# The output projection of a hybrid encoder layer as seven block products in place of eight

## The chip, the core and the metric

The kernel runs on one core of a Trainium2 chip. The metric is device time in microseconds (us) for one execution. The engines are TensorE (PE; PEld is its weight load), VectorE (DVE), ScalarE (ACT), GpSimd (POOL) and SyncE (SP, which issues the transfers). Each works through its own list of instructions in order.

## What is computed

One layer on 1024 tokens of 1024 channels, all in float32. Only the last lines matter here:

```
y_a = attn * silu(z_a)
y_b = h * silu(z_b)
m = sigmoid(g_a + b_merge[0]) * (y_a @ w_ba) + sigmoid(g_b + b_merge[1]) * (y_b @ w_bb)
out = m @ w_out
return layer_norm(ALPHA * x + out, ln_g, ln_b)
```

`y_a` and `y_b` are 1024 x 512, `w_ba` and `w_bb` 512 x 1024, `m` 1024 x 1024 and `w_out` 1024 x 1024.

## The kernel before

A float32 product is made from three products of fp32r numbers. Each operand is split into a high part (a copy, cast to fp32r) and a low part (the rest, by `lo_of`, L127). `mm3` (L130) issues three matmuls for each 128-row piece of the contraction: high x high, low x high, high x low. Nearly every matmul of the kernel has line L134, so one goes by the tile's name.

The kernel has an earlier part (embedding layer norm, input projection, gated recurrence) and the attention, which the change leaves as they are but for the shape of one tile. The order of the instructions on every engine is the order in which the program writes them. What follows attention is this:

**The merge of the branches** (tiles `mb`, loop at L1316). `m` is built transposed: for j = 0..7 (128 channels each) and n = 0, 1 (512 tokens each) a group of twelve matmuls forms 128 x 512 of `y_a @ w_ba` in a PSUM bank. `b_load`, `b_split` fetch and split the weights for the next j (ACT makes the high part, L900, POOL the low one); `g_load` fetches the gate. `merge` (L1300) then lets DVE multiply by the gate (`b_gate`, L1020) and add the other branch's part `late["m", j, n]` (L1302), ACT make the high part `mh` (L1304), and `merge_lo` lets DVE make the low part `ml` one step later. The other branch's part was formed during attention (`filler`), and so its tiles `m` lie in SBUF. Beside that, ACT and POOL split the rows of `w_out` into `wo` (L1344 and L128), 128 x 1024 at a time.

**The output projection** (tiles `o`, `o_product` at L1365, loop at L1390). For each of the eight tiles i of 128 tokens, and for each half of the columns, 24 matmuls (eight k, three each) with `mh` and `ml` as weights and `wo` as the moving operand fill a bank. DVE adds `ALPHA` times the layer's input `z` (L1399) and takes statistics (L1402, L1404). `newton` (L1375) has ACT take a root (L1378) and DVE refine it. For all tiles but the last, ACT then scales `z` (L1408), POOL multiplies by the gain and adds the bias (L1409, L1410), each over 1024 columns, and SP stores the tile (L1411). The last tile's second half is formed in two pieces of 256 columns, and DVE does all of its end (L1416, L1421), with four stores (L1422).

Banks come in turn from eight: two tags `mb`, `s`, `tp` of two banks each, and two banks `acc` of the attention.

## Time and profile before

| | us |
|---|---|
| median of 3 runs (676.55 to 676.87) | 676.69 |
| the profiled execution | 676.07 |
| its span, first to last instruction | 674.3 |

| engine | busy us in the span | share |
|---|---|---|
| PE | 663.7 | 98% |
| DVE | 498.9 | 74% |
| ACT | 364.5 | 54% |
| POOL | 354.4 | 53% |

A row of the profile's groups or of its timeline gives line, engine, operation, the tile written and those read, the shape, and times. In a group's row `busy, mean ns` is followed by the idle time ahead of it and who ended it. In the timeline the first two numbers are the start and the length in us from the span's start, and square brackets hold idle time ahead. Line numbers are those of the kernel before, unless a run of another kernel is shown.

### The profile page before, as it was taken

The page shows a single profiled execution, that of the slowest core. Times are in us where ns is not written, and L with a number is a line of the kernel's source. Part 1 is how long each engine was busy: PE and PEld are TensorE (multiplying, and loading weights), DVE is VectorE, ACT ScalarE, POOL GpSimd, SP SyncE. Part 2 cuts the span into 40 slices and gives each one's busy share as a digit, 9 for nine tenths or more (in the row PEclk, how much of TensorE's full clock was granted, in tenths as well). Part 3 has the DMA queues.
Part 4 walks back from the last instruction along what each step waited for, and adds up shares of the span by engine and source line. Part 5 has one row for each costly group of instructions (what it writes and reads, how often), then busy time and mean ns, then how long its engine had stood idle before and what let it go on. Part 6 is the DMA issues. An engine that isn't in the chain of part 4 may idle for free.

```text
span 674.3 us, 9352 instructions
## 1 busy us (share of the span) xinstructions
PE 663.7 (98%) x3189; PEld 554.3 (82%) x3189; DVE 498.9 (74%) x835; ACT 364.5 (54%) x615; POOL 354.4 (53%) x261
## 2 busy tenths in 40 slices
PE   8999999999999999999999999999999999999995
PEld 7888888888888887888788888888888888888884
DVE  6978876985998699879968785477788787443334
ACT  6555433357786676669576634477777555210110
POOL 5898263433676575567647544115255456334432
PEclk9999999999999999999999999999999999999999
DMA  8746616033344033531543557998794467412211
GB/s 322 246 152 228 209 41 221 36 125 109 126 143 150 22 108 110 172 126 48 202 172 124 172 186 261 339 332 308 251 317 146 163 232 280 170 62 94 93 63 62
DMA packets 48990, 113.40 MB, mean 168 GB/s; under 512 B 5088, under 2 KB 9776, under 8 KB 47408
## 3 DMA queue, kind: packets, MB, share of 16 engines
q1 hardware_dynamic: 48912, 112.81, 48.0%
q8 instruction: 25, 0.41, 0.2%
q14 instruction: 21, 0.17, 0.1%
q10 hardware_dynamic: 32, 0.01, 0.0%
HBM read 77.11 MB, written 35.68 MB: 167 GB/s over the span
## 4 chain that ended last, share of the span: by engine, by line
PE 76%; DVE 9%; issue 4%; POOL 1%; ACT 1%; DMA 1%; SPq 0%; DVEq 0%; POOLq 0%
PE a L134 28%; PE o L134 13%; PE mb L134 13%; PE s L134 11%; PE acc L1145 4%; PE s L1099 3%; PE pt L1121 3%; PE g L794 2%; POOL ht_l L128 1%; DVE ws_l L128 1%; DVE wa_l L128 1%; DMA a_2f<-in_w_s_dram 1%; DVE uc L752 1%; ACT ht_h L312 1%; DVE s_12f L384 0%
## 5 line engine op out<-in xcount | busy, mean ns | idle before, releaser
L134 PE MATMUL a<-ht_h,ws_h 128*128 128x512 f32 x136 | 53.1, 391 | 0.0
L134 PE MATMUL a<-ht_h,ws_l 128*128 128x512 f32 x136 | 53.0, 389 | 0.0
L134 PE MATMUL a<-b_h,wa_l 128*128 128x512 f32 x136 | 53.0, 389 | 0.0
L134 PE MATMUL a<-ht_l,ws_h 128*128 128x512 f32 x136 | 52.9, 389 | 0.0
L134 PE MATMUL a<-b_h,wa_h 128*128 128x512 f32 x136 | 52.9, 389 | 0.0
L134 PE MATMUL a<-b_l,wa_h 128*128 128x512 f32 x136 | 52.9, 389 | 0.0
L134 PE MATMUL o<-wo_h,ml 128*128 128x512 f32 (+1 forms) x136 | 51.2, 377 | 0.0
L134 PE MATMUL o<-wo_l,mh 128*128 128x512 f32 (+1 forms) x136 | 51.2, 376 | 0.0
L134 PE MATMUL o<-wo_h,mh 128*128 128x512 f32 (+1 forms) x136 | 51.2, 376 | 0.0
L1109 DVE CUSTOM_DVE_ANT_0 sc<-s,bias 128x384 f32<-128x384 f32 (+1 forms) x64 | 33.3, 522 | 21.5 <-PE s L1099 14.1
L1399 DVE SCALAR_TENSOR_TENSOR z<-z,o 128x512 f32<-128x512 f32 (+1 forms) x17 | 11.2, 656 | 51.1 <-PE o L134 51.1
L1129 ACT CAST pt_h<-pt 128x384 fp32r<-128x384 f32 x64 | 29.0, 453 | 25.3 <-PE pt L1121 17.3
L1409 POOL TENSOR_TENSOR z<-z,gb 128x1024 f32<-128x1024 f32 x7 | 16.8, 2397 | 48.6 <-ACT z L1408 48.6
L1114 ACT ACTIVATE p<-sc,summ 128x384 f32<-128x384 f32 (+1 forms) x64 | 37.8, 591 | 5.5 <-DVE summ L1109 5.3
L1378 ACT ACTIVATE sd<-mv,eps_z 128x1 f32<-128x1 f32 x8 | 2.4, 294 | 67.1 <-DVE mv L1404 67.1
L128 DVE TENSOR_TENSOR pt_l<-pt,pt_h 128x384 fp32r<-128x384 f32 x64 | 33.2, 519 | 2.1 <-ACT pt_h L1129 1.6
L326 PE MATMUL v<-wv,b_h 128*128 128x512 f32 x128 | 32.8, 398 | 0.2 <-ACT b_h L279 0.2
L902 POOL CAST wb_h<-wb 128x512 fp32r<-128x512 f32 x9 | 7.0, 778 | 49.3 <-DMA wb<-in_w_bb_dram 49.3
L128 POOL TENSOR_TENSOR ht_l<-t,ht_h 128x512 fp32r<-128x512 f32 x16 | 22.0, 1408 | 19.9 <-ACT ht_h L312 19.9
L1099 PE MATMUL s<-ks,qs 128*128 128x384 f32 (+1 forms) x128 | 31.5, 327 | 0.0
L134 PEld LDWEIGHTS a<-ht_h,ws_h 128*128 128x128 f32 x136 | 25.5, 188 | 5.9 <-issue 0.4
L1121 PEld LDWEIGHTS pt<-ident,p 128*128 128x128 f32 x176 | 23.1, 140 | 8.5
(455 smaller groups left out, 2192.4 us busy)
## 6 DMA issues: line engine op xcount, KB each, us to landing
ks<-k_d SPq DMA_DIRECT2D x8, 1024.0 KB, 8.3
h_d<-x SPq DMA_DIRECT2D x8, 512.0 KB, 5.0
v_d<-vs SPq DMA_DIRECT2D x8, 512.0 KB, 3.5
q_d<-q SPq DMA_DIRECT2D x8, 512.0 KB, 3.0
ga_d<-ga SPq DMA_DIRECT2D x16, 256.0 KB, 2.2
gb_d<-gb SPq DMA_DIRECT2D x16, 256.0 KB, 2.4
k_d<-k SPq DMA_DIRECT2D x8, 512.0 KB, 3.4
qs<-q_d SPq DMA_DIRECT2D x8, 512.0 KB, 5.2
```

What stands on the lines that cost most here:

```text
L128: eng.tensor_tensor(lo, full, hi.bitcast(F32), ALU.subtract)
L134: PE.matmul(o, a, b, start=first and i == 0, stop=last and i == len(prods) - 1, skip_group_check=not (first and last))
L326: PE.matmul(vos[i][:], a, wv[kind == "w"][k][:], start=vn[i] == 0, stop=vn[i] == 23)
L794: PE.matmul(o[:, n, :], w[:, 2 * d + b, :], us[b][:, n * HALF:(n + 1) * HALF], start=z == 0, stop=z == 1)
L1099: PE.matmul(o[:, :P * len(near(t))], q[:, t * P:(t + 1) * P], k[:, z, keys], start=z == 0, stop=z == 1)
L1109: V.tensor_tensor_reduce(s[:, :w], o[:, :w], heads[h][2][:, b0:b0 + w], -1.0, 3.0e38, ALU.add, ALU.min, accum_out=sums[h][0][:, t:t + 1])
L1114: A.activation(probs[h % 2][t][:], scs.pop((h, t))[:, :w], AF.Exp, bias=sums[h][0][:, t:t + 1], scale=-1.0, accum_out=sums[h][1][:, t:t + 1])
L1121: PE.transpose(tp[:, n * P:(n + 1) * P], probs[h % 2][t][:, z * P:(z + 1) * P], ident[:])
L1129: A.copy(pt[0][:, span(b)], tps[h, b][:, :P * len(near(b))])
L1145: PE.matmul(acc[g][:, d:d + w], vvs[h // 2][:, b, h % 2, :], pt[:, a:a + w], start=b in (1, 6) and z == 0, stop=z == 1 and b == (4, 7)[g])
L1399: V.scalar_tensor_tensor(z[:, cols], z[:, cols], ALPHA * TWICE, o, ALU.mult, ALU.add)
L1409: G.tensor_tensor(z[:], z[:], gb2[:, 0, :], ALU.mult)
```

## The change

The 1024 x 1024 product is cut into two by two blocks of 512 and done by seven block products (Winograd's form) in place of eight. With A = `m` (rows: two halves of the tokens, columns: two halves of the channels) and B = `w_out`:

- left operands: a11, a12, a22, s1 = a21 + a22, s2 = s1 - a11, s3 = a11 - a21, s4 = a12 - s2
- right operands: b11, b21, b22, t1 = b12 - b11, t2 = b22 - t1, t3 = b22 - b12, t4 = b21 - t2
- products: a11 b11, a12 b21, s2 t2, s1 t1, s4 b22, s3 t3, a22 t4

Each product is done for four pairs p of token tiles (p and p + 4) in turn: a product for one p is twelve matmuls of 512 columns. Two banks serve each p, X and W. DVE reads X after a11 b11, after s2 t2 has been summed in, and again after s3 t3 and a22 t4; W likewise. `z` is now four quarters of 512 columns per pair, to which DVE adds what it reads.

The left sums are formed in the merge: DVE writes s3 over the bank of n = 1 (j < 4), and s2 and s4 over the bank that a22 came from. The right sums t1 to t4 are made by DVE from SBUF pieces of `w_out` of 128 x 512. ACT makes the high parts; the low parts of the right operands and of s1 are POOL's, the others DVE's. The tile `ya` becomes 16 tiles, so that its places can be taken over one by one. Steps are numbered by slots: 0 to 15 are the sixteen groups of the merge, 16 to 43 the 28 products. A table gives the jobs of each slot, which the program writes ahead of that slot's matmuls. The first product's low parts of b21 are in slots 16 to 19; those of t2 in 18 to 21.

A row tile's end (`finished`) now has ACT and POOL work on two halves of 512 columns, with two stores. The last tile's end works in the banks.

```
-    acc = [pst.tile([P, HALF], F32, name=f"acc{g}") for g in range(2)]
+    acc = [pst.tile([P, HALF], F32, tag=f"acc{g}", name=f"acc{g}") for g in range(2)]
...
+    RING = ("mb", "mb", "s", "tp", "acc0", "s", "tp", "acc1")
...
+    def merge(slot):
+        j, n = divmod(slot, 2)
+        c, o, m = j % 4, got[slot], late["m", j, n]
         b_gate(0, j, n, o)
+        if j < 4 and n:
+            V.tensor_tensor(m[:], o[:], m[:], ALU.add)
+            minus(o[:], late["m", j, 0][:], m[:])
+        else:
+            V.tensor_tensor(o[:], o[:], m[:], ALU.add)
+
+    def split(slot):
...
+        if name == "a22":
+            high(name, c, o[:], late["mp"], f"m{j}1")
+            V.tensor_tensor(late["m", c, 1][:], late["m", c, 1][:], o[:], ALU.add)
+        else:
+            high(name, c, o[:], ap, f"{name}h{c}")
+        if n == 0:
+            A.copy(m[:], o[:])
...
+    def second(c, o):
+        minus(o[:], late["m", c, 1][:], late["m", c, 0][:])
+        high("s2", c, o[:], late["mp"], f"m{c}0")
+
+    def fourth(c, o):
+        low("s2", c, o[:], ap, f"s2l{c}")
+        minus(o[:], late["m", c + 4, 0][:], o[:])
+        high("s4", c, o[:], late["mp"], f"m{c + 4}0")
+
+    def fourth_lo(c, o):
+        low("s4", c, o[:], wop, f"s4l{c}")
...
+    for slot in range(16):
+        j, n = divmod(slot, 2)
+        if slot > 1:
+            jobs.setdefault(slot + 1, [])[:0] = [lambda s=slot: merge(s), lambda s=slot: split(s)]
+        job(slot + 2, split_lo, slot)
+        if n and j >= 4:
+            job(slot + 2, lambda c, s: second(c, got[s]), j - 4, slot)
+            job(slot + 3, lambda c, s: fourth(c, got[s]), j - 4, slot)
+            job(slot + 4, lambda c, s: fourth_lo(c, got[s]), j - 4, slot)
...
+    for c in range(4):
...
+        job(2 * c + 3, t1, c)
+        job(2 * c + 4, lambda c: w_high("b11", c, wop, f"b11h{c}"), c)
+        job(2 * c + 5, lambda c: w_low("b11", c, raw["b11", c], wop, f"b11{c}"), c)
...
+        job(16 + c, lambda c: low("b21", c, raw["b21", c][:], yap, f"y1{c}1", G), c)
+        job(16 + c, lambda c: z_load(c, 0, 0, ev, "z", bufs=5), c)
...
+        job(17 + c, t2, c)
+        job(17 + c, t4, c)
+        job(17 + c, lambda c: w_high("t2", c, yap, f"y1{c}0"), c)
+        job(18 + c, lambda c: w_low("t2", c, raw["t2", c], yap, f"y0{c}1"), c)
+        job(18 + c, lambda c: high("s1", c, late["m", c, 1][:], yap, f"y0{c}0"), c)
...
+        job(20 + c, lambda c: w_low("s1", c, late["m", c, 1], late["mp"], f"m{c}1"), c)
+        job(21 + c, t3, c)
...
+    def finished(p, r):
+        mv = mean_var(p, r)
+        sd, ve = newton(mv, f"{p}{r}", iter(()))
+        V.tensor_scalar(ve[:, 2:3], mv[:, 0:1], -1.0, sd[:], ALU.mult, ALU.mult)
+        for n in range(2):
+            z = zs[p, r, n]
             A.activation(z[:], z[:], AF.Identity, bias=ve[:, 2:3], scale=sd[:])
+            G.tensor_tensor(z[:], z[:], gbs[0, n][:], ALU.mult)
+            G.tensor_tensor(z[:], z[:], gbs[1, n][:], ALU.add)
+            SP.dma_start(out[p + 4 * r][:, halves[n]], z[:])
...
+    LAST = [("s3", "t3", 0), ("s3", "t3", 1), ("a22", "t4", 0), ("s3", "t3", 2), ("a22", "t4", 1), ("s3", "t3", 3),
+            ("a22", "t4", 2), ("a22", "t4", 3)]
+    PLAN = [("a11", "b11"), ("a12", "b21"), ("s2", "t2"), ("s1", "t1"), ("s4", "b22")]
+    plan = [(a, b, p) for a, b in PLAN for p in range(4)] + LAST
...
+    for n, (a, b, p) in enumerate(plan[:-1]):
+        jobs.setdefault(17 + n, []).insert(0, lambda a=a, p=p: EVAC[a](p))
```

## The prediction, made before the changed kernel was run

> **What bounds the kernel now.** I read the page's head first, then stages, then the chain of the last stages in order of time.

> ```profile
> span 674.3 us, 9352 instructions
> PE 663.7 (98%) x3189; PEld 554.3 (82%) x3189; DVE 498.9 (74%) x835; ACT 364.5 (54%) x615; POOL 354.4 (53%) x261
> ```

> TensorE is busy for 98% of the span. An average does not say what a change in one stage is worth, so here are the busy times by stage (columns: stretch, length, PE, PEld, DVE, ACT, POOL, granted clock, DMA share, GB/s):

> ```profile
> 535.20:578.80 43.60, 43.60 (x193) 35.98 (x193) 33.97 (x50) 21.37 (x33) 27.78 (x16) 1.00 0.78 278
> 578.80:622.00 43.20, 43.20 (x192) 35.77 (x192) 16.03 (x36) 6.78 (x9) 16.79 (x7) 1.00 0.18 69
> 622.00:666.10 44.10, 44.10 (x218) 37.34 (x216) 16.86 (x43) 6.15 (x8) 19.16 (x8) 1.00 0.20 77
> 666.10:674.30 8.20, 0.02 (x1) 0.00 (x0) 4.79 (x15) 0.29 (x1) 0.00 (x0) 0.80 0.24 80
> ```

> The first row is the attention branch's projection (tiles mb), the next two the output projection (o), the last the tail. In the first, DVE is already busy 34.0 of 43.6 us; in the second and third DVE and POOL have half their time free. The chain of work that ended last, over these stages:

> ```profile
> 535.19 43.59 PE mb L134 x192
> 578.77 87.36 PE o L134 x408
> 666.14 0.02 issue
> 666.16 0.43 DVE z L1399
> ...
> 670.26 0.79 DVE z L1421 x2
> ```

> Nothing but TensorE up to 666.13, then a DVE tail. So matmuls taken out of o are worth their full time, as long as TensorE never waits and the end stays as short.

> **Unit.** 192 matmuls in 43.59 us: 0.227 each. I call twelve of them, 2.724 us, a slot: slots 0 to 15 are mb, and the output projection follows. Its 408 are 360 of 512 columns (81.7 us) and 48 of 256 columns, (87.36 - 81.7) / 48 = 0.118 each.

> **Matmuls removed.** Seven products for four token pairs are 28 slots, 16 to 43; the last is split in halves: 324 x 0.227 + 24 x 0.118 = 76.4 us. That is **-11.0 us**: without a wait, TensorE would end at 655.1.

> **DVE work added in the mb stage.** Before, each slot gives DVE three instructions (gate, add, low part). The changed code adds a difference in the bank for s3, an added right half for a22, two differences and two low parts for s2 and s4, and t1 to t4 from SBUF weights. These rows show what DVE pays:

> ```profile
> 540.53 0.69 DVE L128 TENSOR_TENSOR ya_l<-attn,ya_h 128x512 fp32r<-128x512 f32 x1 [0.69 <-ACT ya_h L1199]
> 541.14 0.69 DVE L1020 SCALAR_TENSOR_TENSOR mb<-g,mb 128x512 f32<-128x512 f32 x1
> 541.86 0.70 DVE L1302 TENSOR_TENSOR mb<-mb,m 128x512 f32<-128x512 f32 x1
> 543.21 0.69 DVE L128 TENSOR_TENSOR ml<-mb,mh 128x512 fp32r<-128x512 f32 x1 [0.66 <-ACT mh L1304]
> ...
> 545.15 0.69 DVE L1020 SCALAR_TENSOR_TENSOR mb<-g,mb 128x512 f32<-128x512 f32 x1
> 545.87 0.70 DVE L1302 TENSOR_TENSOR mb<-mb,m 128x512 f32<-128x512 f32 x1
> 546.48 0.68 DVE L128 TENSOR_TENSOR ml<-mb,mh 128x512 fp32r<-128x512 f32 x1
> 547.07 0.69 DVE L1020 SCALAR_TENSOR_TENSOR mb<-g,mb 128x512 f32<-128x512 f32 x1
> ```

> Start to start, 0.72 us where an instruction uses what the one ahead wrote, 0.60 where not. DVE reaches the first merge at 541.14, with slot 2 running: it begins over 5 us behind, and before it catches up because three instructions take 1.93 of 2.72 us. In the changed order each slot from 2 to 11 has four (about 2.6 us: no catching up), and slots 12 to 17 have 6, 5, 6, 5, 6, 6 (up to 4 us): it falls further behind.

> What waits for it: in the order of the changed kernel, POOL's low part of b21's third block stands behind that of t2's first block, and b21's fourth behind t2's second. t2 comes from DVE behind all of the above, and product a12 x b21 needs b21's fourth low part in its first slot, slot 20. Up to that t2, DVE has 2 + 4 + 9x4 + 28 + 6 + 4 = 80 instructions. 34 gaps have the second using the first's tile (0.72: 24.5 us), 45 do not (27.0), the last lasts 0.69, one early wait for ACT's high part 0.6. That is 52.8 us.

> Fifteen of the 80 read two SBUF tensors. Their collisions with POOL show where both did so before:

> ```profile
> 534.43 2.56 POOL L1183 TENSOR_TENSOR za<-za,rsb 128x512 f32<-128x512 f32 x2 [8.40 <-DMA rsb<-rs_d]
> 536.93 1.76 POOL L128 TENSOR_TENSOR wb_l<-wb,wb_h 128x512 fp32r<-128x512 f32 x1
> 544.72 1.29 POOL L128 TENSOR_TENSOR wb_l<-wb,wb_h 128x512 fp32r<-128x512 f32 x1 [6.03 <-ACT wb_h L900]
> ...
> 535.92 1.61 DVE L1198 TENSOR_TENSOR attn<-attn,za 128x512 f32<-128x512 f32 x1
> ```

> The DVE instruction ended 0.54 after POOL's, at 537.5, having lost 0.92; POOL's next lost 0.47. So one waits for the other's end. Bounds for fifteen: 0 (none meets) to 13.8 us (all lose 0.92). POOL has one instruction per slot in slots 4 to 12 and some at 17 and 18; laying the two queues side by side, six meet, at about 0.45: 2.7 us.

> [...]

> t2's second block is then done at 541.14 + 52.8 + 2.7 = 596.6. ACT's high part (row below), POOL's low part of t2 (1.29) and of b21 (1.29, plus 0.45 for meeting DVE's next difference) bring 600.3. TensorE, unhindered, would want it after eleven matmuls of slot 20: 535.19 + 20 x 2.724 + 11 x 0.227 = 592.2. **+8.1 us.** Some of it appears earlier: the weight split for mb (L900 on ACT, then POOL) now stands behind ACT's high part of s3 in the queue, which waits for DVE, so slots 6 and 14 should lose some 1.7 us each and slot 20 the rest, about 4.5. As DVE never waits for TensorE there, the total is set by DVE's queue. If there are no meetings at all it is 5 us. Then TensorE ends at 600.3 + 0.2 + 22 x 2.724 + 2.8 = 663.3, 2.8 earlier than before.

> ```profile
> L1304 ACT CAST mh<-mb 128x512 fp32r<-128x512 f32 x16 | 9.4, 588 | 20.3 <-DVE mb L1302 20.3
> L900 ACT CAST wb_h<-wb 128x512 fp32r<-128x512 f32 x7 | 4.4, 622 | 0.0
> ```

> ACT gains no more than four casts of 0.6 us per slot, under 2.72; it only passes DVE's lateness on. POOL has two low parts of 1.29 per slot in slots 18 to 29, due four slots or more ahead: covered, unless meetings add over about 4 us.

> **Loads.** The 4 MB of w_out come as 256 KB pieces at a similar pace; the 16 loads of z move from slots 9 on to 16 and later, one slot or more ahead of use, where the DMA share was 0.18. I cost them at nothing. TensorE's slot 17 to 20 cover them; if that fails, DVE's adds shift.

> **The end.** Rows finish in another pattern: four row tiles become ready in slots 33 to 36, three more in 39, 41 and 43. Each needs two multiplies and two adds of 512 columns on POOL, in place of two instructions of 1024. The early rows with this very pattern, and one tile of before from DVE's add to POOL:

> ```profile
> 30.83 5.29 POOL L259 TENSOR_TENSOR x<-x,gb 128x512 f32<-128x512 f32 x4 [1.05 <-ACT x L253]
> ...
> 589.69 0.69 DVE L1399 SCALAR_TENSOR_TENSOR z<-z,o 128x512 f32<-128x512 f32 x1 [4.02 <-PE o L134]
> ...
> 592.72 1.25 ACT L1408 ACTIVATE z<-z,ve,sd 128x1024 f32<-128x1024 f32 x1 [1.04 <-DVE ve L1407]
> ...
> 594.04 2.40 POOL L1409 TENSOR_TENSOR z<-z,gb 128x1024 f32<-128x1024 f32 x1 [12.47 <-ACT z L1408]
> ```

> Seven tiles at 5.25 (5.29 less the overlap) are 36.75 us. From slot 32's end to TensorE's end there are only 10 x 2.724 + 2.8 = 30.05 us. POOL starts 4.35 - 0.55 (half the width on ACT) = 3.8 after slot 32, so it ends 3.8 + 36.75 - 30.05 = 10.5 us after TensorE, at 673.8. At half of a 2.40 instruction (1.20) it would be 33.6 us, 7.4 after. SP keeps its order, so the last tile's four stores, ready near 668, queue behind POOL's last store:

> ```profile
> 669.89 1.79 SPq L1422 DMA_DIRECT2D out_dram<-z  x4
> ```

> Five issues at 0.45, the last at 675.65; before, the last issue (671.35) stood 2.95 ahead of the span's end: 678.6. The tail is thus 15.3 us in place of 8.2: **+7.1**.

> **Sum:** -11.0 + 8.1 + 7.1 = +4.2; rounded, span 678.6, time 676.07 + 4.3 = 680.4. The profiled execution was 0.6 below the median of the runs; I give **680.5**.

> **Rivals.**
> - *DVE keeps up* (faster). If b21's low part lands by 592.2, only the tail is paid: 676.07 - 11.0 + 7.1 = 672.2. DVE's 80 instructions would need 0.595 us each at most with no meeting; faster by over 0.2% needs a total wait under 2.5 us, 0.625 each. The rows' 0.60 and 0.72 speak against. Chance 0.09.
> - *POOL is not the end*: DVE's own tail is (8.2): 673.3. It needs POOL at 1.10 us an instruction; rows show 1.29. 0.04.
> - *No meetings*: 2.7 + 0.45 less: 677.3, within the bound. 0.12.
> - *More waits*: meetings slow POOL's 26 low parts so that slots 24 and 28 wait too: 3 to 4 us more, 684. 0.07.
> - *The clock drops*. After the last matmul the granted clock fell:

> ```profile
> 668.00:670.00 2.00, 0.00 (x0) 0.00 (x0) 2.00 (x7) 0.00 (x0) 0.00 (x0) 1.00 0.00 0
> 670.00:672.00 2.00, 0.00 (x0) 0.00 (x0) 1.05 (x3) 0.00 (x0) 0.00 (x0) 0.73 0.54 176
> 672.00:674.30 2.30, 0.00 (x0) 0.00 (x0) 0.00 (x0) 0.00 (x0) 0.00 (x0) 0.50 0.23 75
> ```

> The fall to half was near 670.9, 4.8 us after the last matmul. Slot 20's longest gap is about 3.5 us, so I expect none; a gap of 4.8 would cost, at half clock for as long, 2.4 us: 682.9. Chance 0.08. [...]

> That seven products are not what is issued is excluded: the changed list holds 60 fewer matmuls, as counted.

> **Chances and range.** Forecast 0.60 (677.9 to 683). 0.2%, 1.35 us, is about what can be told from no change. Faster 0.13 (first two rivals), same 0.12, slower 0.75. Range 675.4 to 684.0: it leaves out the faster cases and about 0.06 above.

> **What would show it.** Right: TensorE waits for wb's low part around slots 6 and 14, and for b21's in slot 20, about 8 us in all; DVE without a gap from 541 to about 608; POOL back to back over the last 36 us, ending some 10 us after TensorE, with the last four stores behind it. Wrong: no waits on TensorE ahead of slot 21, or a chain that ends on DVE; waits for z or weights by DMA, which I cost at nothing.

## The result, and the profile after

| | before | changed |
|---|---|---|
| median of 4 runs, us | 676.66 (676.55 to 676.87) | 686.37 (685.94 to 687.03) |
| profiled execution, its span | 676.07, 674.3 | 686.13, 684.3 |

The changed kernel is slower: ratio 1.0144, 95% interval 1.0126 to 1.0162. Forecast were 680.5 us and a range up to 684.0. The sign was right, and the time lies above the range.

The head of the changed kernel's page:

```profile
span 684.3 us, 9463 instructions
...
PE 658.1 (96%) x3129; PEld 545.7 (80%) x3129; DVE 535.9 (78%) x888; ACT 384.8 (56%) x662; POOL 383.0 (56%) x299
```

60 matmuls fewer, and yet PE is busy for only 5.6 us less, partly since some matmuls ran at half clock (0.43 us from start to start behind 604.86, in place of 0.227). The stages, with the same columns as before:

```profile
535.20:578.80 43.60, 40.45 (x175) 31.77 (x173) 39.06 (x57) 20.29 (x37) 17.43 (x13) 1.00 0.69 236
...
601.00:604.00 3.00, 0.00 (x0) 0.00 (x0) 2.90 (x5) 1.99 (x4) 2.88 (x2) 1.00 0.00 0
604.00:607.00 3.00, 2.88 (x8) 2.29 (x9) 2.91 (x4) 1.30 (x4) 2.92 (x3) 0.58 0.00 0
...
672.00:684.30 12.30, 0.00 (x0) 0.00 (x0) 3.32 (x11) 0.00 (x0) 7.12 (x6) 0.53 0.36 128
```

TensorE has holes in the merge (40.45 of 43.6 us; it was full before), stands still from 601 to 604 while DVE and POOL are busy for nearly all of it, and then runs 3 us at a granted clock of 0.58. What TensorE waited for, in sum, number and longest, and where:

```profile
PE w L134 <- POOL b21l L128: 3.6, 2, 3.4
PE mb L134 <- ACT wb_h L900: 2.3, 2, 1.4
PE mb L134 <- POOL wb_l L128: 1.7, 2, 0.9
```

```profile
578.41 0.49 PE L134 MATMUL mb<-ya,wb_h 128*128 128x512 f32 x1 [0.85 <-ACT wb_h L900]
579.76 0.50 PE L134 MATMUL mb<-ya,wb_l 128*128 128x512 f32 x1 [0.85 <-POOL wb_l L128]
...
604.12 0.52 PE L134 MATMUL w<-b21l,a12h 128*128 128x512 f32 x1 [3.38 <-POOL b21l L128]
```

These are the tiles and slots of the forecast (6, 14 and 20), 7.6 us in sum against "about 8". That match is of the gaps alone. By the times from one matmul's start to the next, the six waits cost 8.8 us, and matmuls that ran at half clock behind slot 14 or started up again behind a wait (0.33 us to the next start behind 579.76 and 604.12) some 2.5 more, so TensorE was about 11 us late in slot 20. The queue behind the last wait, on DVE and then POOL:

```profile
542.15 0.69 DVE L1021 SCALAR_TENSOR_TENSOR mb<-g,mb 128x512 f32<-128x512 f32 x1
...
544.72 0.69 DVE L128 TENSOR_TENSOR a11l<-mb,a11h 128x512 fp32r<-128x512 f32 x1 [1.14 <-ACT m L1346]
...
569.10 0.69 DVE L1342 TENSOR_TENSOR m<-m,mb 128x512 f32<-128x512 f32 x1 [0.65 <-ACT a22h L1317]
...
598.82 1.45 DVE L1324 TENSOR_TENSOR t<-wb,t 128x512 f32<-128x512 f32 x1
```

```profile
597.18 1.30 POOL L128 TENSOR_TENSOR t2l<-t,t2h 128x512 fp32r<-128x512 f32 x1 [9.72 <-ACT t2h L1317]
...
602.35 1.71 POOL L128 TENSOR_TENSOR b21l<-wb,b21h 128x512 fp32r<-128x512 f32 x1
...
678.09 1.26 POOL L1490 TENSOR_TENSOR z<-z,gb 128x512 f32<-128x512 f32 x1
```

t2's second block (598.82) ends at 600.27, where 596.6 was forecast; b21's fourth low part ends at 604.06, where 600.3 was. TensorE's last matmul ends at 668.95 (forecast 663.3), POOL's last addition 10.4 us after it (10.5), the span 15.35 after it (15.3). SP's own queue shows why the span goes on after POOL: the last tile's four stores are issued behind POOL's last store.

```profile
645.53 34.18 SPq L1491 DMA_DIRECT2D out_dram<-z  x14
679.80 1.86 SPq L1594 DMA_DIRECT2D out_dram<-z  x4
```

So three facts carry the difference: a loss of about 11 us up to slot 20, a stretch at half clock behind it, and a tail that is about 7 us longer. The experiments take them one by one.

### The profile page after: what moved, and what is told of

Its sections match the earlier page's. It is cut to its first block, busy times and chain, and to the rows that moved or that the text cites. A ratio compares the mean times of both kernels' runs of the same rounds, so it can differ in the third digit from the quotient of the medians.

```text
span 684.3 us, 9463 instructions
## 1 busy us (share of the span) xinstructions
PE 658.1 (96%) x3129; PEld 545.7 (80%) x3129; DVE 535.9 (78%) x888; ACT 384.8 (56%) x662; POOL 383.0 (56%) x299
## 5 line engine op out<-in xcount | busy, mean ns | idle before, releaser
L134 PE MATMUL a<-ht_h,ws_h 128*128 128x512 f32 x136 | 53.1, 391 | 0.0
L134 PE MATMUL a<-ht_h,ws_l 128*128 128x512 f32 x136 | 53.0, 390 | 0.0
L134 PE MATMUL a<-b_h,wa_l 128*128 128x512 f32 x136 | 53.0, 389 | 0.0
L134 PE MATMUL a<-b_h,wa_h 128*128 128x512 f32 x136 | 52.9, 389 | 0.0
L134 PE MATMUL a<-ht_l,ws_h 128*128 128x512 f32 x136 | 52.9, 389 | 0.0
L134 PE MATMUL a<-b_l,wa_h 128*128 128x512 f32 x136 | 52.9, 389 | 0.0
L134 PE MATMUL mb<-ya,wb_h 128*128 128x512 f32 x128 | 41.4, 402 | 2.3 <-ACT wb_h L900 2.3
L128 POOL TENSOR_TENSOR wb_l<-wb,wb_h 128x512 fp32r<-128x512 f32 x16 | 21.9, 1372 | 26.6 <-ACT wb_h L900 25.9
L128 DVE TENSOR_TENSOR pt_l<-pt,pt_h 128x384 fp32r<-128x384 f32 x64 | 33.2, 519 | 2.1 <-ACT pt_h L1131 1.6
L128 POOL TENSOR_TENSOR ht_l<-t,ht_h 128x512 fp32r<-128x512 f32 x16 | 22.0, 1404 | 19.9 <-ACT ht_h L312 19.9
L134 PEld LDWEIGHTS mb<-ya,wb_h 128*128 128x128 f32 x128 | 24.8, 194 | 8.5 <-ACT wb_h L900 3.1
L134 PEld LDWEIGHTS a<-ht_h,ws_h 128*128 128x128 f32 x136 | 25.5, 188 | 6.0 <-issue 0.5
L134 PEld LDWEIGHTS a<-b_h,wa_h 128*128 128x128 f32 x136 | 25.5, 188 | 5.4
L134 PEld LDWEIGHTS a<-ht_l,ws_h 128*128 128x128 f32 x136 | 25.5, 188 | 5.4
L134 PEld LDWEIGHTS a<-b_l,wa_h 128*128 128x128 f32 x136 | 25.5, 188 | 5.3
```

The costliest lines, as they stand in the source:

```text
L128: eng.tensor_tensor(lo, full, hi.bitcast(F32), ALU.subtract)
L134: PE.matmul(o, a, b, start=first and i == 0, stop=last and i == len(prods) - 1, skip_group_check=not (first and last))
```

## The experiments

All are edits of the changed kernel. A gain in the text is the changed kernel's ratio 1.0144 less the run's ratio to the kernel before, times 676.66; a ratio compares runs on one chip. As both ratios have an interval, a gain is uncertain by about 1.6 us either way.

Some expectations speak of a lock of DVE and POOL. The changed kernel's trace shows this of it, from 541 to 611: nine times a DVE instruction on two SBUF tensors began while one of POOL's ran, and each ended 0.54 to 0.56 us after POOL's end (1.45 us in all at 598.82, where one undisturbed takes 0.69); eight times one of POOL's began while such a one of DVE's ran, and ended 1.12 to 1.17 us after it (1.71 at 602.35; 1.29 undisturbed). At 598.22 a DVE instruction that reads a bank kept its 0.68 beside POOL. What makes one wait for the other, no run shows.

**1. b21's low parts ahead of t2's.**

```
-        job(16 + c, lambda c: low("b21", c, ...
+        job(16, lambda c: low("b21", c, ...
```

> One edit: all four low parts of b21 stand in POOL's queue ahead of t2's, so none of them is behind a difference that DVE forms late. Theory (the wait in slot 20 is one of order: b21's fourth low part behind t2's second block, and t2 behind DVE's queue): TensorE's wait there (0.19, 0.52 and 3.38 us) goes, the stretch at half clock after it (604 to 607.9) goes with it, and about 1 us comes back as a wait for t1's low part around slot 28. TensorE ends near 662.5 in place of 668.9, POOL's last addition and the last store move up by the same: 686.4 - 6.5 = 679.9 us. Rival (DVE's queue is the bound wherever the wait shows, so t2 or t1 is late next by as much): under 1.5 us gained, 685 or more, with waits of 3 us or more for t2l or t1l in slots 24 to 31. Second rival (the clock's fall has nothing to do with the wait): a stretch at half clock stays near 604, and only 4.2 us are gained, 682.1.

Measured: 680.32 us, ratio 1.0057 (1.0042 to 1.0072), a gain of 5.9 us. Slot 20 has no wait and no half clock; what is late next is a small wait in slot 28:

```profile
PE w L134 <- POOL t1l L128: 1.6, 1, 1.6
```

So the wait of slot 20 was one of order: POOL could have made all of b21's low parts 12 us earlier (the last ends at 591.87 here, at 604.06 in the changed kernel), in time that it spent idle for t2 (9.72 us ahead of 597.18, shown above). Both rivals fall.

**2. Half of POOL's tail left out.**

```
+            if n == 0:
-            G.tensor_tensor(z[:], z[:], gbs[0, n][:], ALU.mult)
-            G.tensor_tensor(z[:], z[:], gbs[1, n][:], ALU.add)
+                G.tensor_tensor(z[:], z[:], gbs[0, n][:], ALU.mult)
+                G.tensor_tensor(z[:], z[:], gbs[1, n][:], ALU.add)
```

> Leaves work out: the seven row tiles that POOL finishes get gain and bias in their left half only (14 of POOL's 28 last instructions are gone). Theory (the end is set by POOL's queue of 28 instructions of about 1.3 us, which begins when slot 32 is done): POOL's last instruction comes no later than DVE's tail of the last tile, the span ends about 8 us after TensorE in place of 15.4, and the time is 686.4 - 7 = 679.4 us; TensorE still ends near 668.9. Rival (stores or DVE's own tail hold the end, POOL merely runs beside it): under 1 us gained, 685.5 or more.

Measured: 681.28 us, ratio 1.007 (1.0055 to 1.0085), a gain of 5.0 us. The forecast was 679.4. TensorE ends at 669.15, the span at 678.9, 9.75 later. POOL now waits for ACT, and the chain that ends last is DVE's work on the last tile:

```profile
670.63 1.27 POOL L1490 TENSOR_TENSOR z<-z,gb 128x512 f32<-128x512 f32 x1 [3.05 <-ACT z L1488]
```

```profile
674.74 0.78 DVE z L1594 x2
```

POOL's queue is thus 5.6 us (15.35 less 9.75) of the 7.1 that the tail grew by. The other 1.6 are the last tile's own end, 9.75 us in place of 8.2: the rival "POOL is not the end" had that at 8.2 still.

**3. TensorE kept busy in the wait of slot 20.** `x` and `y` are the operands of product a12 b21, p = 0:

```
+                if i == 11:
+                    for _ in range(13):
+                        PE.matmul(o, zero_w[:], hi[b, 0][:], start=False, stop=False, ...)
+                PE.matmul(o, x[:, rows], y[:], start=i == 0, stop=i == 11, ...)
```

> Adds work: 13 matmuls with zero weights in slot 20, ahead of the matmul that waits for b21's fourth low part, so that TensorE is busy for 2.95 us of its 3.4 us there; they add zero to the bank. Theory (the stretch at half clock from 604.1 to 607.9 comes from the idleness just ahead of it and costs 16 or 17 matmuls 0.2 us each, twice 1.8 with its edges counted once): with TensorE busy up to about a microsecond before, the clock stays at 1.00 there, and TensorE ends 1.8 us earlier although it has 13 matmuls more: 684.6 us. Rival (the clock falls by what the chip draws or by the earlier stretch at 580 to 584, not by this gap): the half-clock stretch stays, 686.4 us or up to 1 us more.

Measured: 684.49 us, ratio 1.0114 (1.0097 to 1.0131), a gain of 2.0 us with 13 matmuls more. The thirteen, the wait that is left, and the stage that was at 0.58 (columns as above):

```profile
600.03 3.12 PE L1543 MATMUL w<-b21h,zero_w 128*128 128x512 f32 x13
603.62 0.50 PE L1544 MATMUL w<-b21l,a12h 128*128 128x512 f32 x1 [0.47 <-POOL b21l L128]
```

```profile
604.00:607.00 3.00, 3.00 (x15) 2.47 (x14) 2.91 (x4) 1.26 (x4) 2.90 (x2) 1.00 0.00 0
```

The half clock came from TensorE's idleness (with the wait filled the stage is at 1.00 in place of 0.58), and costs about 1.7 us behind slot 20: from the matmul that waited to TensorE's end it is 64.8 us in the changed kernel (604.12 to 668.95) and 63.2 here (603.62 to 666.85). In this execution the clock did not fall behind slot 14 either, but that is not the gain: the matmul in slot 20 comes only 0.5 us earlier.

**4. DVE's sum ahead of ACT's high part.**

```
+            V.tensor_tensor(late["m", c, 1][:], late["m", c, 1][:], o[:], ALU.add)
             high(name, c, o[:], late["mp"], f"m{j}1")
-            V.tensor_tensor(late["m", c, 1][:], late["m", c, 1][:], o[:], ALU.add)
```

> One edit: in slots 9, 11, 13 and 15 DVE's right-half sum for a22 is issued ahead of ACT's high part of the same bank, so DVE no longer waits for ACT to have read it. Theory (DVE's queue up to t2 sets slot 20's wait, and four waits of 0.65 us on ACT were left out of the forecast's 80 instructions): DVE's second t2 block is done about 2.4 us earlier (near 597.9 in place of 600.3), TensorE's wait in slot 20 is shorter by that, 686.4 - 2.4 = 684.0 us; if the shorter gap (about 1 us) lets the clock stay at 1.00, a further 1.8 us go: 682.2. Rival (DVE waits elsewhere as long, for ACT's high part or a lock, so the four waits were no loss): 686 us or more, t2 done within 0.5 us of 600.3.

Measured: 683.06 us, ratio 1.0097 (1.008 to 1.0113), a gain of 3.2 us. The same sum has no wait now, and t2's second block ends at 597.31:

```profile
567.90 0.69 DVE L1341 TENSOR_TENSOR m<-m,mb 128x512 f32<-128x512 f32 x1
...
595.86 1.45 DVE L1324 TENSOR_TENSOR t<-wb,t 128x512 f32<-128x512 f32 x1
```

That is 3.0 us earlier, of which 0.6 are an earlier start of this execution (DVE's first merge at 541.56 in place of 542.15), so the four waits were worth the 2.4 expected. ACT's high part now waits for DVE in turn:

```profile
574.26 0.59 ACT L1317 CAST a22h<-mb 128x512 fp32r<-128x512 f32 x1 [0.94 <-DVE m L1341]
```

The longest wait in slot 20 is 3.38 still, set by the distance of two low parts on POOL, with half clock behind it; but the matmul that ends it starts at 601.16 in place of 604.12.

**5. The weights of the merge split earlier.**

```
+        if 2 < slot < 16 and n == 0:
+            b_split(0, j + 1, A)
         for f in jobs.pop(slot, ()):
...
-            if n == 0 and j > 0:
-                b_split(0, j + 1, A)
+            if slot == 2:
+                b_split(0, 2, A)
```

> One edit: in slots 4 to 14 the split of the next projection weight (ACT's high part, POOL's low part) is issued ahead of the merge of the slot before, so ACT's high part no longer stands behind one that waits for DVE. Theory (TensorE's four waits in slots 6 and 14, 4.0 us in sum, are only early instalments of DVE's lateness, since DVE hardly ever waits for TensorE there): these waits go, slot 20's waits grow from 3.6 us by most of it, and the time stays within 684.0 to 686.4 us (about 2 us may come from locks that DVE and POOL now meet in another pattern). Rival (the four waits are paid in full): 686.4 - 4.0 = 682.4 us, with slot 20's waits as they were.

Measured: 685.59 us, ratio 1.0145 (1.0131 to 1.0159): no gain by ratio. Three of the four early waits are gone, and slot 20 has them:

```profile
PE w L134 <- POOL b21l L128: 8.6, 2, 5.9
```

The forecast's sentence that the total is set by DVE's queue holds: taking away the waits that one sees first gains nothing.

**6. Row tiles whole two slots earlier.**

```
-    plan = [(a, b, p) for a, b in PLAN for p in range(4)] + LAST
+    plan = [(a, b, p) for a, b in PLAN[:3] for p in range(4)]
+    plan += [(*PLAN[3 + s], p) for s, p in ((0, 0), (0, 1), (1, 0), (0, 2),
+                                            (1, 1), (0, 3), (1, 2), (1, 3))] + LAST
```

> One edit, in the order of products only: s1 x t1 and s4 x b22 are interleaved in slots 28 to 35, so that the first row tile is whole after slot 30 instead of 32; every instruction stays. Theory (the tail is POOL's 28 instructions from the first whole tile on, and POOL stands idle for 5.7 us ahead of the first of them): POOL's queue starts up to 5.4 us earlier, ends about 7 us after TensorE in place of 10.4, and the time is 686.4 - 3.6 = 682.8 us, TensorE's end staying at 668.9. Rival (POOL's low parts for t3 and t4 fill the idle time, or TensorE has to wait for b22's low part that is now due two slots earlier): under 1 us gained, 685.5 or more.

Measured: 682.51 us, ratio 1.0103 (1.0089 to 1.0118), a gain of 2.8 us. POOL's first gain is at 637.45 (642.84 in the changed kernel) and its last addition ends at 675.66, 6.7 us after TensorE in place of 10.4. The mechanism has the size expected: the profiled executions differ by 3.7 us (686.13 and 682.46), where 3.6 were forecast, and the 2.8 by ratio is no different from that within its uncertainty.

**7. Three edits to the queues together** (those of 1 and 4, and `t1` by `G.tensor_tensor` in place of `minus`).

> Three edits to the queues together: b21's low parts ahead of t2's on POOL, the right-half sum for a22 ahead of ACT's high part, and the four t1 differences on POOL instead of DVE. Theory (what TensorE loses is DVE's queue and the order on POOL): no wait in slot 20 or later, no stretch at half clock there, TensorE ends near 659.7 (only the waits at slots 6 and 14 are left, some 3 us), POOL ends 10 us after it, and the time is 686.4 - 9.3 = 677.1 us. Rival (the gains are not additive, since POOL now has the t1 differences and its locks with DVE): as the first edit alone, 680.3 us.

Measured: 677.15 us, ratio 1.0022 (1.0013 to 1.0031), a gain of 8.3 us of the 9.3 expected. The rival falls: the gains of 1 and 4, 9.1 us in sum, add within the noise. What moving `t1` gives by itself is not shown. TensorE ends at 660.5; the waits at slots 6 and 14 and 0.4 us in slot 28 are left, with one stretch at half clock after slot 6.

**8. All edits.** Besides 5, 6 and 7:

```
+        if n:
             low(name, j % 4, got[slot][:], ap, f"{name}l{j % 4}")
+        else:
+            low(name, j % 4, late["m", j, 0][:], ap, f"{name}l{j % 4}", G)
...
-        SP.dma_start(out[p + 4][:, halves[n]][:, part], z[:, part])
+        A.dma_start(out[p + 4][:, halves[n]][:, part], z[:, part])
```

> All edits that keep the seven products: the three of the run on queues, the early weight split, the interleaved order of products, four plus four low parts of a11 and a12 moved from DVE to POOL (from the SBUF copy of the bank), and the last tile's four stores issued by ACT instead of behind POOL's stores on SP. Theory (-11.0 us of matmuls are there to be had; what is in the way are DVE's queue and POOL's tail): TensorE waits 2 us in all, ends near 658.5, the span ends 10 to 12 us after it, and the time is 672.5 us (670.5 to 674.5), faster than the kernel before by 0.3 to 0.9%. Rival (POOL, with 8 more low parts, becomes what TensorE waits for in slots 4 to 16 or 24 to 31): 677 us or more.

Measured: 671.14 us, ratio 0.9935 (0.9923 to 0.9947): faster than both kernels, and a little better than expected. 2.2 us of waits are left (1.74 for t1's low part, 0.5 for t2's), with one stretch at half clock behind the longer one. The rival falls.

**9. The same with a filled wait** (as in 3, five matmuls in the first product s1 t1).

> The kernel of all edits with five zero-weight matmuls (they add zero) in slot 28, ahead of the matmul that waits 1.74 us there for t1's fourth low part. Theory (half speed comes in whole stretches of 3.41 us on a fixed grid, one after each stretch of the grid in which TensorE idled half the time or more; a lone wait of 1.74 us was enough there): the wait is cut to some 0.6 us, the clock stays at 1.00 through 616 to 621, and 1.7 us go: 671.1 - 1.7 = 669.4 us. Rival (the fall there has another cause, such as the chip's draw or the load of POOL and TensorE together): the stretch at half clock stays and the time is 671.1 us or up to 0.5 us more.

Measured: 672.03 us, ratio 0.9943 (0.9929 to 0.9956). The time of neither theory: it did not get shorter. The clock stayed at 1.00 and TensorE's last matmul ended at 658.3, 0.9 us earlier than in run 8, though the merge began 0.6 later in this execution. But POOL's last addition did not follow:

```profile
665.59 1.26 POOL L1493 TENSOR_TENSOR z<-z,gb 128x512 f32<-128x512 f32 x1
```

It ends at 666.85, 8.5 us after TensorE. In run 8 it ended at 666.15. From 603 on POOL has no gap in either, so in both its queue set the end, and TensorE's gain had nowhere to go.

**10 and 11. POOL relieved, without and with the fill.**

```
-        job(28 + c, lambda c: w_low("t4", c, raw["t4", c], wop, f"b21{c}"), c)
+        job(31 + c, lambda c: w_low("t4", c, raw["t4", c], wop, f"b21{c}", eng=V), c)
```

> The kernel of all edits with one more: t4's four low parts are DVE's, three slots later, since POOL had no gap there from 603 to its last addition at 666 and DVE was idle for half of that time. Theory (in the kernel of all edits POOL's queue sets the end, and TensorE's end with the last tile's own tail stands right behind it, 0.5 us earlier): POOL ends about 2 us earlier, but only 0.4 us are gained: 671.1 - 0.4 = 670.7 us. Rival (POOL alone sets the end): 669.1 us. If DVE's four instructions make it late for the banks: 672 us or more.

> The same with five zero-weight matmuls in slot 28 as in the run before (they add zero). Theory (the half-clock stretch there costs 1.7 us of TensorE's time, which could not show while POOL's queue set the end): with POOL relieved it shows, TensorE ends 1.5 us earlier than without the fill and the time is 1.3 to 1.7 us below that of the kernel without it: near 669.2 us. Rival (the fill gains nothing in any case, for a reason not seen yet): as without it or up to 1 us more, 670.7 to 671.7 us.

Measured: 670.98 us (669.1 to 673.11, ratio 0.9921, 0.9903 to 0.994) without the fill, 670.47 us (669.65 to 670.9, ratio 0.9914, 0.9902 to 0.9927) with it. Both beat the kernel before; the two can't be told apart. The median of the first is as forecast, but by luck: three of its six executions took 669.1 to 669.8 us, three 672.2 to 673.1, none near 670.7. The second gained less than expected. The profile of 10 shows why it is no clean test: its wait in slot 28 is that of run 8, but the clock did not fall. First run 8's wait and the stretch behind it, then those of run 10:

```profile
616.13 0.50 PE L134 MATMUL w<-t1l,s1h 128*128 128x512 f32 x1 [1.74 <-POOL t1l L128]
```

```profile
616.60:620.00 3.40, 3.40 (x10) 2.62 (x9) 0.69 (x1) 0.00 (x0) 3.24 (x3) 0.50 0.02 5
```

```profile
615.60 0.50 PE L134 MATMUL w<-t1l,s1h 128*128 128x512 f32 x1 [1.68 <-POOL t1l L128]
```

```profile
612.00:616.00 4.00, 2.32 (x11) 1.59 (x10) 0.13 (x1) 0.00 (x0) 3.76 (x4) 1.00 0.01 2
616.00:620.00 4.00, 4.00 (x19) 3.31 (x18) 1.38 (x2) 0.00 (x0) 3.77 (x4) 1.00 0.01 4
```

The same gap costs a stretch in one execution and none in the other. Falls of the clock within one execution lie on a grid of 3.41 us where they were read off here (last section), and behind the last matmul of 10 it fell near 662.06:

```profile
662.00:663.00 1.00, 0.00 (x0) 0.00 (x0) 1.00 (x4) 0.00 (x0) 0.92 (x2) 0.53 0.67 250
```

Fourteen steps back (47.78 us by experiment 6's two falls), such a grid runs through 614.28, which cuts this gap (613.92 to 615.60) into 0.36 and 1.32 us; run 8's gap lay whole in one step. That the runs of 10 spread over 4.0 us and those of 11 over 1.25 fits with such a draw. So does the mean granted clock, 0.996 in the three shorter executions of 10 and 0.993 to 0.994 in the longer ones; but that mean also counts when the clock falls behind the last matmul, and the executions without a profile were not followed through time, so what the fill is worth on average stays open.

## Why the prediction was right in sign and short in size

Term by term, in the profiled executions (686.13 - 676.07 = +10.1):

| term | forecast | measured |
|---|---|---|
| matmuls removed | -11.0 | -11.0: 60 fewer, and outside the half-clock stretches one takes 0.227 as before |
| start of slot 0 | 0 | +0.7 (535.75; 535.03 before) |
| DVE's queue up to slot 20 | +8.1 | +11.4: b21's fourth low part was wanted at 592.7 (535.75 + 20 x 2.724 + 11 x 0.227) and used at 604.12 |
| half clock after slot 20 | 0 | +1.7 (3.41 us at half clock; experiment 3 gains 2.0) |
| tail | +7.1 | +7.2 (15.35 - 8.2) |

The profiled execution lies 5.7 us above the forecast (686.13 against 680.4): 3.3 by the queue, 1.7 by the clock, 0.7 by the start of slot 0. The start differs between executions, 534.3 to 535.8 over all profiles here, and is not shown to be the change's doing.

- **The place and the chain of the wait were right.** Slots 6, 14 and 20 wait for the tiles named; experiment 5 shows that the early waits are instalments, 1 that the last is one of POOL's order, 4 that DVE's queue sets it.
- **The failed step is the length of that queue**: "Up to that t2, DVE has 2 + 4 + 9x4 + 28 + 6 + 4 = 80 instructions ... one early wait for ACT's high part 0.6. That is 52.8 us." The start-to-start times of 0.72 and 0.60 hold. Missing were four waits of 0.65 for ACT:

```profile
DVE m L1342 <- ACT a22h L1317: 2.6, 4, 0.7
```

  Both instructions only read the bank, so on data alone neither waits for the other; but in this kernel the one that comes second in the program waits for the first (DVE for ACT here, 0.65 us; ACT for DVE in experiment 4, 0.94 us), and the diff puts ACT's first. Experiment 4 shows the 2.4 us. The early wait was 1.14 and not 0.6, also behind a second ACT reader (the copy, L1346); and the queue began at 542.15 and not 541.14, of which 0.7 is slot 0's own later start. Together 4.1; against them the meetings with POOL came to some 0.4 less than the 2.7 allowed (the longest at 598.82, 1.45 for 0.69).
- **The clock rival was wrongly shut out.** "The fall to half was near 670.9, 4.8 us after the last matmul. Slot 20's longest gap is about 3.5 us, so I expect none." One fall after a long idle time gives a bound from above for the idle time needed, not the idle time itself. The gap was 3.38 us and the clock fell; two gaps of 0.85 us were enough as well (last section). The rival was given 0.08; as an even case at 1.7 us it would have taken the upper end of the range from 684.0 to about 686.
- **The tail was right** in sum, and the reason for 5.6 of its 7.2 us: POOL's 28 instructions. Experiment 6 moves their start and with it the end.
- **"DVE keeps up"** gave 672.2 us for a kernel in which only the tail is paid. Experiment 8, with the tail shortened as well, comes to 671.14: the matmuls removed are a real gain, spent nearly twice over on queues and the clock.

## What to carry to other kernels

When TensorE gets less work, count the instructions of the engine that feeds it up to each tile that TensorE needs, with one wait for every bank that a second engine also reads where the trace has such waits (four of 0.65 us here), and look in what order the low parts stand behind it. A wait seen early can be an instalment of a late one: take away the cause on the engine behind, and then look which queue runs to the end without a gap, since a gain elsewhere does not pass it. And a wait of TensorE can have a price beyond its length, in the matmuls behind it (1.7 us behind slot 20's here).

## What the runs showed of the hardware

```profile
580.00:581.00 1.00, 1.00 (x5) 0.77 (x5) 0.97 (x3) 0.20 (x1) 0.00 (x0) 0.78 0.42 154
581.00:582.00 1.00, 1.00 (x4) 0.81 (x3) 0.97 (x3) 0.95 (x2) 0.00 (x0) 0.50 0.00 0
582.00:583.00 1.00, 1.00 (x4) 0.80 (x3) 0.35 (x2) 0.74 (x2) 0.00 (x0) 0.50 0.00 0
583.00:584.00 1.00, 1.00 (x4) 0.71 (x3) 1.00 (x2) 0.00 (x0) 0.00 (x0) 0.51 0.00 0
...
604.00:605.00 1.00, 0.88 (x3) 0.75 (x4) 1.00 (x2) 0.69 (x2) 1.00 (x2) 0.73 0.00 0
605.00:606.00 1.00, 1.00 (x4) 0.81 (x3) 1.00 (x2) 0.00 (x0) 0.92 (x2) 0.50 0.00 0
606.00:607.00 1.00, 1.00 (x4) 0.72 (x4) 0.91 (x2) 0.61 (x2) 1.00 (x1) 0.50 0.00 0
607.00:608.00 1.00, 1.00 (x4) 0.81 (x3) 1.00 (x2) 1.00 (x4) 0.92 (x2) 0.57 0.00 0
```

Twice what the slices lack of 1.00 is the length: (0.22 + 0.50 + 0.50 + 0.49) x 2 = 3.42, and 3.40 for the second. By the same sum it was 3.40 to 3.42 in experiments 1, 4, 7 and 8 and behind slot 6 in 6, and 6.82 after slot 20 in experiments 2 and 6 and 10.24 in 5: multiples of 3.41. The falls lie on a grid, too: here at 580.56 and 604.46, 23.90 apart, which is 7 x 3.41; in experiment 6 at 553.52 and 601.30 (its slices below), 14 x 3.41.

```profile
553.00:554.00 1.00, 0.48 (x1) 0.49 (x2) 1.00 (x2) 0.49 (x2) 1.00 (x2) 0.76 0.82 231
...
601.00:602.00 1.00, 0.00 (x0) 0.00 (x0) 1.00 (x3) 0.58 (x2) 1.00 (x2) 0.65 0.00 0
```

How long TensorE was idle in the step of the grid ahead of a fall varied. In the changed kernel the step ahead of 580.56 held the two gaps of slot 14, 1.70 us of 3.41, and the clock fell; of slot 6's gaps (1.44 and 0.85) 1.43 fell into one step, and it did not. In experiment 6 slot 6's gaps were no longer (1.15 and 0.86), but lay in one step, 2.0 us, and it did. Experiment 8's lone gap of 1.74 made it fall. Experiment 1's gap of 1.63 in slot 28 lay whole in one step (620.0 to 623.4, counted from that run's fall at 555.15), and it did not. So here 1.70 us of a step was enough in two pieces, 1.74 in one, and 1.63 was not. That is no border: behind the last matmul of experiments 8 and 9, whose end is modelled, 1.77 and 1.73 us of a step were idle, and the clock fell only at the end of the next. "Half the time or more", in the expectation of experiment 9, was thus the author's estimate, and what sets the grid no run shows. Whether a gap of 1.7 us was followed by a stretch at half clock, 1.7 us more, went here with where it fell on the grid (experiments 8 and 10), and that differs between executions.
